# Decay exponents of a chunked delta rule: from broadcast loads and GpSimd products to sums by TensorE in PSUM

## The chip, the cores and the metric

The kernel runs on one core of a Trainium2 chip. The time is device microseconds of one launch. Three runs of the kernel before gave 1200.51, 1200.98 and 1204.93 us; the median, 1200.98 us, is the time before. One more execution was recorded by the hardware profiler: its own time is 1201.35 us, and its trace spans 1199.4 us.

## The reference, cut to what matters

One encoder layer runs over a prompt of 512 tokens and a sample of 256, each behind 16 meta tokens. The mixer has two branches: an attention branch with latent projections, and a gated delta rule that runs forward and backward over chunks of 64 tokens. A feed-forward part follows. All is float32. The change touches only the preparation of the delta rule's chunk matrices:

```python
gc = jnp.cumsum(g, axis=-1)
decay = jnp.exp(jnp.where(tri, gc[..., :, None] - gc[..., None, :], -jnp.inf))
m = jnp.where(strict, jnp.einsum('bhncd,bhnsd->bhncs', kb, k) * decay, 0.0)
attn = jnp.einsum('bhncd,bhnsd->bhncs', q, k) * decay
qg = q * jnp.exp(gc)[..., None]
```

For each chunk, head and direction a 64 x 64 matrix of differences of cumulated gates is needed, masked to a triangle and exponentiated. It multiplies k k^T (for the triangular system) and q k^T (for the local attention). q is scaled by exp(gc) as well.

## The kernel before, in words

The sequence (14 chunks of 64 columns, prompt and sample together) lies along the free axis, 128 features along the partitions. Two heads share a tile, so four pairs j = 0..3 cover the eight heads (`for j in range(NPB)`). Every float32 product of the large projections is three float32r products of a high and a low part (`proj`, L331: 48 matmuls of 384 or 400 columns per tile of 128 output features; `split`, L212 and L213, makes the parts of a weight, on ScalarE and VectorE).

The stage around the change works so, for each pair j:

- `conv` (L449 to 469) projects k and q of the pair into one two-bank PSUM tile each (pool `d2`, two tiles), ScalarE copies them to `xb`, and three VectorE steps (L465) convolve them, the result back in the same PSUM tile. `silu_pad` then applies SiLU on ScalarE (the function table is loaded again for each change between SiLU and exp/log, L184). Only then is the `d2` tile free for the next projection.
- `l2` squares (L485 on GpSimd for k, L487 on VectorE for q), sums over a head with a float32 matmul (L492, into a bank of pool `b`, three banks), and normalizes (L498, L500) to `kq`. `tokens` transposes k and stores it.
- For each half (seven chunks): two loads (L542) broadcast five lines from DRAM (`gD`: gc forward, gc backward, -beta forward, and gc of both directions with the heads swapped) over 64 partitions each, into the tile `x3` (the trace calls it x). VectorE subtracts gc of the row (L547, L548), GpSimd adds the masks (L549, L550), ScalarE takes exp of three matrices and of the two lines `en`, GpSimd multiplies by -beta (L553), VectorE by the backward one (L554). These are the four matrices `dc`.
- A matmul per chunk (L561) gives k k^T and q k^T; VectorE multiplies them by `dc` into `LT` (L566) and `ua` (L569), GpSimd multiplies `en` and q into `ua` (L568), and `ua` is stored to `UD` (L571), in two parts per half.

The lines in `gD` are made before, after the gates (L413 to 423): three times a copy, a transpose on TensorE (L417), a copy to SBUF (L419) and stores.

After the stage `LT` is transposed to `LP` (L585, L587), and 30 steps of a sequential inverse run on VectorE (`inv_steps`, L596, L598). Meanwhile the four v and four z projections (`vtok`, `zgate`) and then five latent ones go through TensorE. The v convolution writes to an SBUF tile `y` (three buffers). Then a scan over the chunks, attention, output projection and feed-forward follow.

The order on each engine isn't written by hand: a planner orders the instructions when the kernel is built, by program order as priority and by its own estimate of when each is ready, and every engine then keeps its order. All DMAs of these stages are issued by one queue, SyncE's (SP). A tile is waited for before its memory is used again, also where a later pool takes over an earlier pool's memory.

Of the kernel before, what the change touches and what calls it, by code (L numbers as in the profile page):

```python
# [5 lines left out]
F32 = mybir.dt.float32  # L6
# [27 lines left out]
def lay_consts():  # L34
    i = np.arange(128)
    c = {}
    c["ident"] = np.eye(128)
    c["J"] = np.tile(np.eye(64), (2, 1))
    c["bd1"] = np.kron(np.eye(2), np.ones((64, 64)))
    c["one"] = np.ones((128, 128))  # L40
    p = (i % 64)[:, None]
    f = np.arange(64)[None, :]
    c["tf"] = (p <= f) * 1.0
    c["tb"] = (p >= f) * 1.0
    c["nf"] = np.where(p <= f, 0.0, NEG)
    c["nb"] = np.where(p >= f, 0.0, NEG)
    s = np.zeros((128, 128))
    for m in range(128):
        r = m % 32
        s[r, m] = 1.0  # L50
        if r < 16:
            s[32 + r + 16, m] = -1.0
        else:
            s[32 + r - 16, m] = 1.0
    c["sk"] = s
    c["hm"] = np.kron(np.eye(8), np.ones((16, 64)))
    names, cols, arrs = [], {}, []
# [24 lines left out]
_C, _CC = lay_consts()


def lay(inp):

    a = {}
    a["x"] = np.concatenate([inp["meta_tokens"], inp["x_prompt"][0], inp["x_sample"][0]], 0)
    w = inp["w_in"][0]
    cq, ckv, kr, q, k, v, z, g = (np.s_[0:384], np.s_[384:640], np.s_[640:672], np.s_[672:1184],  # L90
                                  np.s_[1184:1696], np.s_[1696:2208], np.s_[2208:2720], np.s_[2720:2752])
    tiles = [np.concatenate([w[:, kr], w[:, kr], w[:, g], np.zeros((D, 32), w.dtype)], 1)]
    for j in range(4):
# [44 lines left out]
def body(ctx, tc, I, O):  # L138
# [26 lines left out]
    def bank(n="b"):  # L165
        return banks[n].tile([P, 512], F32, name=n, tag=n)
# [3 lines left out]

    def bank2():
        return banks["d2"].tile([P, 2, 512], F32, name="d2", tag="d2")
    banks_set(b=3, c=1, d2=2)

    def pool(es, name, bufs, side="right", **kw):
        return es.enter_context(tc.tile_pool(name=name, bufs=bufs, side=side, reuse_waits="tile", **kw))
# [232 lines left out]

    nbT = gqp.tile([P, 2, NCH, 4], F32, name="nbT")  # L410
    V.tensor_scalar_mul(nbT, bT, -1.0)
    gD = dp.tile([2, 5, 56, 64], F32, name="gD")
    for i, src in enumerate((gcT[:, 0], gcT[:, 1], nbT[:, 0])):  # L413
        ps = bank()
        cj = gp.tile([P, 4, NCH], F32, name="cj")
        V.tensor_copy(cj, src.rearrange("p c j -> p j c"))
        T.transpose(ps[:56, :P], cj.rearrange("p j c -> p (j c)"), ident)  # L417
        row = gp.tile([56, P], F32, name="row", bufs=2)
        S.copy(row, ps[:56, :P])  # L419
        st(gD[:, i].rearrange("h n c -> n h c"), row.rearrange("n (h c) -> n h c", h=2))  # L420
        if i < 2:
            for h in range(2):
                st(gD[h, 3 + i], row[:, (1 - h) * 64:(1 - h) * 64 + 64])
    egk = gqp.tile([P, 2, NCH, 4], F32, name="egk")
    act(egk, gcT, AF.Exp)
    ekd = gqp.tile([P, 2, NCH, 4], F32, name="ekd")
    V.tensor_sub(ekd, glT, gcT)
    act(ekd, ekd, AF.Exp)
# [18 lines left out]
    cnt = [0]  # L447

    def ytile():  # L449
        return cvp.tile([P, 803], F32, name="y", tag="y", bufs=3)  # L450

    def conv(ti, wi, eng=V, ceng=V):

# [27 lines left out]

    def l2(ks, out, scale):
        sq = sp.tile([P, GC], F32, name="sq")
        if scale is None:
            G.tensor_mul(sq, ks, ks)  # L485
        else:
            V.tensor_mul(sq, ks, ks)  # L487
        k3 = ks.rearrange("p (n c) -> p n c", c=64)
        for s in range(2):
            ps = bank()  # L490
# [34 lines left out]
    for j in range(NPB):  # L525
# [7 lines left out]
        for half in range(2):  # L533
            n0 = half * 7
            ch = slice(n0, n0 + 7)
            rows = slice(j * NCH + n0, j * NCH + n0 + 7)

            x3 = sp.tile([P, 5, 7, 64], F32, name="x3", bufs=2)
            en = x3[:, 3:5]
            for h in range(2):  # L540
                hr = slice(h * 64, h * 64 + 64)
                ld(x3[hr].rearrange("p r n c -> p r (n c)"),  # L542
                   gD[h, :, rows].rearrange("r n c -> r (n c)").partition_broadcast(64))

            dc = sp.tile([P, 4, 7, 64], F32, name="dc", bufs=2)
            gc = bc(gcT[:, :, ch, j], 3, 64)
            V.tensor_sub(dc[:, 1:4:2], x3[:, 0:2], gc)  # L547
            V.tensor_sub(dc[:, 2], gc[:, 1], x3[:, 1])  # L548
            G.tensor_add(dc[:, 1:3], dc[:, 1:3], bc(bc(C("nf"), 1, 7), 1, 2))  # L549
            G.tensor_add(dc[:, 3], dc[:, 3], bc(C("nb"), 1, 7))  # L550
            act(dc[:, 1:4], dc[:, 1:4], AF.Exp)
            act(en, en, AF.Exp)
            G.tensor_mul(dc[:, 0], x3[:, 2], dc[:, 1])  # L553
            V.tensor_mul(dc[:, 2], dc[:, 2], bc(nbT[:, 1, ch, j], 2, 64))  # L554
            b = bds[half]
            S.copy(b[0:64, :, 64:128], kq[0:64, 0, ch, :])
            S.copy(b[64:128, :, 0:64], kq[64:128, 0, ch, :])
            for a, w in ((0, 4), (4, 3)):
# [5 lines left out]
                sl = slice(a, a + w)  # L564
                nj = slice((n0 + a) * 4 + j, (n0 + a + w - 1) * 4 + j + 1, 4)
                V.tensor_mul(LT[:, :, nj, :], bc(p4[:, 0], 1, 2), dc[:, 0:4:2, sl])  # L566
                ua = sp.tile([P, 2, 4, 2, 64], F32, name="ua", bufs=3)
                G.tensor_mul(ua[:, :, :w, 0, :], en[:, :, sl], bc(kq[:, 1, n0 + a:n0 + a + w, :], 1, 2))  # L568
                V.tensor_mul(ua[:, :, :w, 1, :], bc(p4[:, 1], 1, 2), dc[:, 1:4:2, sl])  # L569
                for r in range(2):  # L570
                    st(UD[r, n0 + a:n0 + a + w, :, j].rearrange("n p i c -> p n (i c)"), ua[:, r, :w].rearrange("p n i c -> p n (i c)"))  # L571
    es.close()
    vp = pool(ec, "vp", 1)

    ei = ExitStack()
# [787 lines left out]
```

## Time and profile before

| | us |
|---|---|
| median of three runs | 1200.98 |
| the profiled execution's own time | 1201.35 |
| its span in the trace | 1199.4 |
| TensorE busy (matmuls) | 1123.9 (94%) |
| VectorE busy | 831.6 (69%) |
| ScalarE busy | 598.9 (50%) |
| GpSimd busy | 156.6 (13%) |

The shares are means over stages with different limits. A matmul's busy time holds its way through the array, so that neighbours overlap: the pace of a row of matmuls is read from the distance of their starts. The stage of the change lies between about 64 and 205 us, and the inverse follows up to 300 us. "Idle" of an engine is put down to what ended it.

### The profile page before, as it was taken

How to read it: one execution, taken by the hardware profiler on the slowest of the kernel's cores; microseconds unless marked ns; L12 is line 12 of the kernel's file. 1: busy time of each engine (PE TensorE's matmuls, PEld its weight loads, DVE VectorE, ACT ScalarE, POOL GpSimd, SP SyncE). 2: the span in 40 equal slices, each digit the busy share in tenths (PEclk: the TensorE clock that was granted, in tenths of full speed). 3: DMA queues.
4: the chain of work that ended last, by engine and by line, in shares of the span. 5: the costliest groups of instructions: out<-in, count | busy, mean ns of one | idle time of the engine just before them, and what ended most of it. 6: DMA issues, size and time to landing. Idle time of an engine off the chain costs nothing.

```text
span 1199.4 us, 18635 instructions
## 1 busy us (share of the span) xinstructions
PE 1123.9 (94%) x7116; PEld 974.5 (81%) x7116; DVE 831.6 (69%) x1358; ACT 598.9 (50%) x1054; POOL 156.6 (13%) x195
## 2 busy tenths in 40 slices
PE   5978888998999899998999899999998999999997
PEld 4877788998889876664677789999998888888885
DVE  7567668689677768778648699777764764494446
ACT  5475664333745656656534566555553533343330
POOL 2134465004513211000000000000000000000000
PEclk9998899999899989899999899999999999999999
DMA  5157764530478764334103025333324875566521
GB/s 209 50 117 182 196 171 130 126 113 31 146 253 238 214 188 124 102 98 158 45 18 106 18 71 179 129 123 123 124 88 145 306 229 177 176 206 203 179 91 52
DMA packets 107962, 168.94 MB, mean 141 GB/s; under 512 B 36242, under 2 KB 72850, under 8 KB 107874
## 3 DMA queue, kind: packets, MB, share of 16 engines
q1 hardware_dynamic: 107874, 167.76, 45.7%
q8 instruction: 56, 0.92, 0.3%
q14 instruction: 32, 0.26, 0.1%
HBM read 128.61 MB, written 39.11 MB: 140 GB/s over the span
## 4 chain that ended last, share of the span: by engine, by line
PE 77%; DVE 9%; DMA 6%; ACT 4%; issue 2%; SPq 1%; POOL 1%; DVEq 0%; ACTq 0%; POOLq 0%
PE w L1326 15%; PE w L1084 10%; PE b L1084 9%; PE d L331 7%; PE b L1326 7%; PE b L1146 5%; PE d L977 3%; PE c L1008 3%; DMA x<-gD 3%; PE b L837 2%; PE d L704 2%; PE b L853 2%; PE v L1005 2%; PE b L877 2%; PE b L870 2%
## 5 line engine op out<-in xcount | busy, mean ns | idle before, releaser
L1326 PE MATMUL w<-w2h,fh 128*128 128x512 f32 x768 | 185.1, 391 | 3.8 <-ACT fh L212 3.8
L1326 PEld LDWEIGHTS w<-w2h,fh 128*128 128x128 f32 x768 | 144.9, 189 | 34.3 <-ACT fh L212 4.1
L331 PE MATMUL d<-hTh,wl 128*128 128x384 f32 (+1 forms) x352 | 123.9, 352 | 3.3 <-DVE wl L213 3.3
L331 PE MATMUL d<-hTh,wh 128*128 128x384 f32 (+1 forms) x352 | 125.1, 355 | 1.4 <-ACT ks L188 1.4
L331 PE MATMUL d<-hTl,wh 128*128 128x384 f32 (+1 forms) x352 | 125.1, 355 | 0.0
L213 DVE TENSOR_TENSOR w2h<-LT,w2h 128x1024 fp32r<-128x1024 f32 x64 | 77.6, 1224 | 48.7 <-ACT w2h L212 48.7
L212 ACT CAST w2h<-LT 128x1024 fp32r<-128x1024 f32 x64 | 66.6, 1049 | 75.4 <-PE b L1326 28.8
L1326 PE MATMUL b<-w2h,fh 128*128 128x512 f32 x384 | 96.4, 389 | 0.0
L1326 PEld LDWEIGHTS b<-w2h,fh 128*128 128x128 f32 x384 | 72.3, 188 | 15.1
L331 PEld LDWEIGHTS d<-hTh,wh 128*128 128x128 f32 x352 | 67.6, 192 | 5.8 <-issue 3.3
L331 PEld LDWEIGHTS d<-hTh,wl 128*128 128x128 f32 x352 | 67.6, 192 | 5.8 <-DVE wl L213 3.7
L331 PEld LDWEIGHTS d<-hTl,wh 128*128 128x128 f32 x352 | 67.6, 192 | 2.6 <-issue 1.5
L213 DVE TENSOR_TENSOR fh<-fr,fh 128x768 fp32r<-128x768 f32 x32 | 30.5, 957 | 55.9 <-ACT fh L212 55.9
L212 ACT CAST fh<-fr 128x768 fp32r<-128x768 f32 x32 | 26.7, 839 | 76.0 <-PE w L1326 38.7
L212 ACT CAST w1h<-LT 128x512 fp32r<-128x512 f32 x50 | 30.8, 620 | 41.2 <-PE w L1084 20.9
L1146 PE MATMUL b<-woh,mh 128*128 128x512 f32 x96 | 42.2, 448 | 5.2 <-ACT woh L212 3.1
L977 PE MATMUL d<-kt,q 128*128 128x512 f32 (+1 forms) x96 | 46.6, 582 | 0.3 <-ACT p L188 0.2
L213 DVE TENSOR_TENSOR w1l<-LT,w1h 128x512 fp32r<-128x512 f32 x50 | 34.4, 689 | 12.6 <-ACT w1h L212 12.6
L1008 PE MATMUL c<-pt,vt 128*64 128x512 f32 (+3 forms) x96 | 42.2, 536 | 0.6 <-ACT pt L1007 0.6
L857 DVE TENSOR_TENSOR YZ<-U,b 64x512 f32<-64x512 f32 x52 | 35.5, 683 | 7.6 <-PE b L853 6.9
L834 ACT COPY YZ<-U 64x512 f32<-64x512 f32 x52 | 32.1, 617 | 17.3 <-issue 11.3
L978 DVE TENSOR_REDUCE mx<-d 128x1 f32<-128x512 f32 (+1 forms) x48 | 28.7, 599 | 16.7 <-PE d L977 16.5
(473 smaller groups left out, 2810.4 us busy)
## 6 DMA issues: line engine op xcount, KB each, us to landing
LT<-in_w_ff SPq DMA_DIRECT2D x85, 512.0 KB, 3.8
FD<-LT SPq DMA_DIRECT2D x16, 768.0 KB, 3.7
fr<-FD SPq DMA_DIRECT2D x32, 384.0 KB, 3.7
wr<-in_w_in SPq DMA_DIRECT2D x22, 512.0 KB, 3.5
x<-gD SPq DMA_DIRECT2D x16, 560.0 KB, 6.2
KV<-vD SPq DMA_DIRECT2D x26, 256.0 KB
U<-UD SPq DMA_DIRECT2D x26, 256.0 KB, 5.3
w1x<-in_w_ff SPq DMA_DIRECT2D x12, 512.0 KB, 4.5
```

The source lines that it names most:

```text
L212: S.copy(hi, src)
L213: return (eng or V).tensor_sub(lo, src, hi.bitcast(F32))
L331: T.matmul(ps[:, s, :c1 - c0], lhsT=a[:, k, :], rhs=b[:, k, c0:c1], start=(k == 0 and i == 0), stop=(k == KT - 1 and i == 2))
L704: T.matmul(ps[:, s, :HR], lhsT=a[:, k], rhs=b[:, cs], start=(k == 0 and i == 0), stop=(k == 2 and i == 2))
L834: S.copy(YZ[h][rows], U[rows, :, :, 1])
L857: V.tensor_sub(YZ[h][rows], U[rows, :, :, 0], wv[rows])
L977: T.matmul(ps[:, :w], lhsT=q[:, qs], rhs=kt[:, k0:k0 + w], start=True, stop=True)
L978: V.tensor_reduce(mx[:, 0, t:t + 1], ps[:, :w], AX.X, ALU.max)
L1008: T.matmul(po[:m, :nq], lhsT=Vs[j][:, t0 + bi, :m], rhs=pt[:, :nq], start=(bi == 0), stop=(bi == ntl - 1))
L1084: x = T.matmul(ps[:, :HR], lhsT=a[:, k, :], rhs=b[:, k, :], start=(k == 0 and i == 0), stop=(k == HQ - 1 and i == 2))
L1146: outp = T.matmul(ps, lhsT=x[:, k, :], rhs=y[:, cs], start=(k == 0 and i == 0), stop=(k == 3 and i == 2))
L1326: T.matmul(po[g][h], lhsT=a[:, i_, qs], rhs=b[:, cs], start=(n_ == 0 and j == 0), stop=(n_ == len(seq) - 1 and j == 2))
```

## The change

The lines go to DRAM as high and low float32r parts: gc of both directions, -beta forward, and now exp(gc) of both directions (`RD`, one store in place of seven). They are loaded once, not per half: `Rw` (20 lines of pair j at partitions 32j) and `Lc` (for each direction the column values of a chunk on 14 partitions, and below them an identity). Constants `dk` hold masks, signs and head selectors and are loaded once and cast. `spread` then forms each matrix of a half in a PSUM bank: for an exponent one matmul with `Lc` (its identity rows add the mask, its other rows add or subtract gc of one index) and one with selector and `Rw` (gc of the other index); for -beta and the two exp(gc) the second alone. So 6 banks and 9 matmuls of 448 columns per half. ScalarE takes exp straight from the bank, VectorE multiplies from the bank. GpSimd has no products here any more; the square of k goes to VectorE. `UD` is stored once per direction and half. Pool `b` has four banks during this stage in place of three and one of pool `c`, and the tile `y` of the v convolution moves from the pool `cvp` to `vp`, which is opened after this stage's pool is closed and takes its memory.

```diff
+def lay_decay():
+    i = np.arange(64)
+    nf = np.tile(np.where(i[:, None] <= i[None, :], 0.0, NEG), (1, 7))
+    nb = np.tile(np.where(i[:, None] >= i[None, :], 0.0, NEG), (1, 7))
+    band = np.tile(np.kron(np.eye(7), np.ones((1, 64))), (2, 1))
+    out = []
+    for sg, m in ((-1.0, nf), (1.0, nf), (-1.0, nb)):
+        a = np.zeros((128, 448))
+        a[:14] = sg * band
+        a[64:] = m
+        out.append(a)
...
-    banks_set(b=3, c=1, d2=2)
+    banks_set(d2=2, b=4)
...
-    gD = dp.tile([2, 5, 56, 64], F32, name="gD")
-    for i, src in enumerate((gcT[:, 0], gcT[:, 1], nbT[:, 0])):
...
+    RD = dp.tile([10, 2, 56, 64], F32, name="RD")
+    rows_ = gp.tile([56, 10, P], F32, name="rows_")
+    for q, src in enumerate((gcT[:, 0], gcT[:, 1], nbT[:, 0], egk[:, 0], egk[:, 1])):
+        if q % 2 == 0:
+            ps = bank()
+        src = src.rearrange("p c j -> p j c")
+        rh = gp.tile([P, 2, 4, NCH], F32R, name="rh", bufs=2)
+        V.tensor_copy(rh[:, 0], src)
+        V.tensor_sub(rh[:, 1], src, rh[:, 0].bitcast(F32))
+        for hl in range(2):
+            o = (q % 2 * 2 + hl) * P
+            T.transpose(ps[:56, o:o + P], rh[:, hl].rearrange("p j c -> p (j c)").bitcast(F32), ident)
+        if q % 2 or q == 4:
+            w = 4 if q % 2 else 2
+            S.copy(rows_[:, q // 2 * 4:q // 2 * 4 + w], ps[:56, :w * P].rearrange("n (r c) -> n r c", c=P))
+    st(RD.rearrange("r h n c -> n r h c"), rows_.rearrange("n r (h c) -> n r h c", h=2))
...
-        return cvp.tile([P, 803], F32, name="y", tag="y", bufs=3)
+        return vp.tile([P, 803], F32, name="y", tag="y", bufs=3)
...
+    dk = sp.tile([P, _D.shape[1]], F32R, name="dk")
+    for c0, c1 in ((0, 1472), (1472, 2240)):
+        raw = sp.tile([P, 1792], F32, name="dc", bufs=2)
+        ld(raw[:, :c1 - c0], I["decay"][:, c0:c1])
+        S.copy(dk[:, c0:c1], raw[:, :c1 - c0])
...
+    raw = sp.tile([P, 1792], F32, name="ua", bufs=2)[:, :896]
+    G.memset(raw, 0.0)
+    for j in range(NPB):
+        ld(raw[32 * j:32 * j + 20], RD.rearrange("r h (j n) c -> j (r h) (n c)", j=4)[j])
+    V.tensor_copy(Rw, raw)
+    for d in range(2):
+        raw = sp.tile([P, 1792], F32, name="ua", bufs=2)[:, :1024].rearrange("p (b c) -> p b c", b=8)
+        G.memset(raw, 0.0)
+        for hl in range(2):
+            for h in range(2):
+                ld(raw[hl * 7:hl * 7 + 7, :, h * 64:h * 64 + 64], RD[d * 2 + hl, h].rearrange("(b n) c -> n b c", n=7))
+        V.tensor_copy(Lc[d][0:64], raw[0:64])
+        S.copy(Lc[d][64:128], bc(dk[64:128, 1344:1472].bitcast(F32), 1, 8))
...
-        if scale is None:
-            G.tensor_mul(sq, ks, ks)
-        else:
-            V.tensor_mul(sq, ks, ks)
+        V.tensor_mul(sq, ks, ks)
...
-            V.tensor_sub(dc[:, 1:4:2], x3[:, 0:2], gc)
-            V.tensor_sub(dc[:, 2], gc[:, 1], x3[:, 1])
-            G.tensor_add(dc[:, 1:3], dc[:, 1:3], bc(bc(C("nf"), 1, 7), 1, 2))
-            G.tensor_add(dc[:, 3], dc[:, 3], bc(C("nb"), 1, 7))
-            act(dc[:, 1:4], dc[:, 1:4], AF.Exp)
-            act(en, en, AF.Exp)
-            G.tensor_mul(dc[:, 0], x3[:, 2], dc[:, 1])
+            def spread(i, d=None, r=None):
+                ps = bank()
+                if d is not None:
+                    T.matmul(ps[:, :448], lhsT=Lc[d][:, 2 * j + half, :], rhs=dkr[r], start=True, stop=False)
+                T.matmul(ps[:, :448], lhsT=dks[i][rs_], rhs=Rw[rs_, half * 448:half * 448 + 448],
+                         start=d is None, stop=True)
+                return ps[:, :448].rearrange("p (n c) -> p n c", c=64)
...
+            act(dc[:, 1], spread(0, 0, 0), AF.Exp)
+            V.tensor_mul(dc[:, 0], dc[:, 1], spread(3))
+            act(dc[:, 2], spread(2, 1, 1), AF.Exp)
             V.tensor_mul(dc[:, 2], dc[:, 2], bc(nbT[:, 1, ch, j], 2, 64))
+            act(dc[:, 3], spread(1, 1, 2), AF.Exp)
+            ua = sp.tile([P, 1792], F32, name="ua", bufs=2).rearrange("p (r n i c) -> p r n i c", r=2, n=7, c=64)
+            for r in range(2):
+                V.tensor_mul(ua[:, r, :, 0, :], kq[:, 1, ch, :], spread(4 + r))
...
-                G.tensor_mul(ua[:, :, :w, 0, :], en[:, :, sl], bc(kq[:, 1, n0 + a:n0 + a + w, :], 1, 2))
-                V.tensor_mul(ua[:, :, :w, 1, :], bc(p4[:, 1], 1, 2), dc[:, 1:4:2, sl])
-                for r in range(2):
-                    st(UD[r, n0 + a:n0 + a + w, :, j].rearrange("n p i c -> p n (i c)"), ua[:, r, :w].rearrange("p n i c -> p n (i c)"))
+                V.tensor_mul(ua[:, :, sl, 1, :], bc(p4[:, 1], 1, 2), dc[:, 1:4:2, sl])
+            for r in range(2):
+                st(UD[r, n0:n0 + 7, :, j].rearrange("n p i c -> p n (i c)"), ua[:, r].rearrange("p n i c -> p n (i c)"))
     es.close()
+    banks_set(d2=2, b=3, c=1)
     vp = pool(ec, "vp", 1)
```

## Rows read from the trace of the kernel before

**Rows 1.** Busy time of each engine by stretch, granted clock, DMA share; columns named first.
```profile
core 0: us, PE busy (x) PEld busy (x) DVE busy (x) ACT busy (x) POOL busy (x), PEclk, DMA share, GB/s
64.00:205.00 141.00, 119.63 (x622) 109.28 (x622) 100.30 (x118) 87.39 (x149) 72.60 (x56) 0.90 0.67 163
205.00:262.00 57.00, 57.00 (x353) 56.70 (x352) 40.37 (x54) 21.28 (x36) 5.56 (x15) 1.00 0.48 125
262.00:300.00 38.00, 34.80 (x194) 33.90 (x192) 37.10 (x40) 13.58 (x22) 13.18 (x14) 1.00 0.14 46
300.00:420.00 120.00, 111.39 (x1706) 103.28 (x1706) 86.09 (x135) 70.48 (x134) 40.09 (x62) 0.96 0.70 213
```
**Rows 2.** Chain that ended last, 40 to 350 us, in order of time.
```profile
64.31 2.20 DMA gD<-row
68.55 12.69 DMA x<-gD
```
**Rows 3.** Waits between 64 and 205 us: us in total, times, longest.
```profile
DVE dc L547 <- DMA x<-gD: 23.3, 7, 6.6
ACT x L188 <- DMA x<-gD: 9.5, 5, 2.9
```
**Rows 4.** TensorE in order of time: starts that give the pace of 384 and 400 columns.
```profile
102.51 0.33 PE L331 MATMUL d<-hTl,wh 128*128 128x384 f32 x1
...
105.82 0.34 PE L331 MATMUL d<-hTh,wl 128*128 128x384 f32 x1
...
106.36 0.34 PE L331 MATMUL d<-hTl,wh 128*128 128x400 f32 x1
...
109.63 0.34 PE L331 MATMUL d<-hTl,wh 128*128 128x400 f32 x1
```
**Rows 5.** Groups of TensorE, 64 to 205 us: busy us, mean ns, idle before.
```profile
L561 PE MATMUL b<-kq,bd 128*128 128x128 f32 x112 | 19.9, 341 | 3.8 <-DVE ua L569 1.5 <-DVE kq L498 1.4 <-ACT kt L508 0.9
L492 PE MATMUL b<-sq,cst 128*128 128x448 f32 x32 | 15.2, 567 | 2.5 <-DVE kq L500 2.5
```
**Rows 6.** Groups of VectorE, 64 to 205 us.
```profile
L213 DVE TENSOR_TENSOR wl<-wr,wh 128x1024 fp32r<-128x1024 f32 x8 | 16.2, 2022 | 1.3 <-ACT wh L212 1.3
L465 DVE SCALAR_TENSOR_TENSOR y<-xb,cols,y 128x803 f32<-128x803 f32 x9 | 10.9, 1212 | 0.3 <-ACT y L462 0.2
L554 DVE TENSOR_TENSOR dc<-dc,nbT 128x448 f32<-128x448 f32 x8 | 10.0, 1251 | 3.5 <-ACT dc L188 3.4
L547 DVE TENSOR_TENSOR dc<-x,gcT 128x896 f32<-128x896 f32 x8 | 8.7, 1092 | 25.2 <-DMA x<-gD 23.3 <-issue 1.9
L548 DVE TENSOR_TENSOR dc<-gcT,x 128x448 f32<-128x448 f32 x8 | 5.2, 644 | 0.0
```
**Rows 7.** VectorE in order of time: single instructions at either duration, and LT's last.
```profile
88.02 0.61 DVE L554 TENSOR_TENSOR dc<-dc,nbT 128x448 f32<-128x448 f32 x1
...
123.24 1.21 DVE L213 TENSOR_TENSOR wl<-wr,wh 128x1024 fp32r<-128x1024 f32 x1
...
154.03 0.61 DVE L498 SCALAR_TENSOR_TENSOR kq<-ks,b 128x448 f32<-128x448 f32 x1
...
202.22 0.55 DVE L566 TENSOR_TENSOR LT<-b,dc 128x384 f32<-128x384 f32 x1
```
**Rows 8.** Groups of ScalarE, 64 to 205 us.
```profile
L188 ACT ACTIVATE dc<-dc 128x1344 f32<-128x1344 f32 x8 | 10.6, 1323 | 1.8 <-POOL dc L549 1.7
L188 ACT ACTIVATE b<-b 128x448 f32<-128x448 f32 x16 | 8.4, 542 | 0.0
L188 ACT ACTIVATE x<-x 128x896 f32<-128x896 f32 x8 | 7.7, 956 | 9.5 <-DMA x<-gD 9.5
```
**Rows 9.** DMA issues, 64 to 205 us: count, KB each, median us to landing.
```profile
x<-gD SPq DMA_DIRECT2D x16, 560.0 KB, 6.2
vD<-kt SPq DMA_DIRECT2D x16, 112.0 KB, 4.8
```
**Rows 10.** TensorE in order of time: the sums for one q tile.
```profile
141.99 1.67 PE L492 MATMUL b<-sq,cst 128*128 128x448 f32 x4
```

More of the change, by code (lines that the diff above doesn't have):

```diff
@@ L44, in lay_consts @@
     c["tb"] = (p >= f) * 1.0
-    c["nf"] = np.where(p <= f, 0.0, NEG)
-    c["nb"] = np.where(p >= f, 0.0, NEG)
     s = np.zeros((128, 128))
@@ L63, in lay_consts @@
     return np.concatenate(arrs, 1).astype(np.float32), cols
+def lay_decay():
[9 more added lines that the diff above has]
+        out.append(a)
+    a = np.zeros((128, 128))
+    a[64:] = np.tile(np.eye(64), (1, 2))
+    out.append(a)
+    head = np.arange(128) // 64
+    for q, sg, swap in ((0, 1.0, 0), (1, 1.0, 0), (1, -1.0, 0), (2, 1.0, 0), (3, 1.0, 1), (4, 1.0, 1)):
+        a = np.zeros((128, 128))
+        for j in range(4):
+            for hl in range(2):
+                for h in range(2):
+                    a[32 * j + (q * 2 + hl) * 2 + h] = sg * (head == (1 - h if swap else h))
+        out.append(a)
+    return np.concatenate(out, 1).astype(np.float32)
 def rope_tables():
@@ L82 @@
 _C, _CC = lay_consts()
+_D = lay_decay()
 def lay(inp):
@@ L124, in lay @@
     a["consts"] = _C
+    a["decay"] = _D
     a["rope"] = rope_tables()
@@ L411, in body @@
     V.tensor_scalar_mul(nbT, bT, -1.0)
-    gD = dp.tile([2, 5, 56, 64], F32, name="gD")
-    for i, src in enumerate((gcT[:, 0], gcT[:, 1], nbT[:, 0])):
[L414 to L423, printed above, removed]
     egk = gqp.tile([P, 2, NCH, 4], F32, name="egk")
     act(egk, gcT, AF.Exp)
+    RD = dp.tile([10, 2, 56, 64], F32, name="RD")
[14 more added lines that the diff above has]
+    st(RD.rearrange("r h n c -> n r h c"), rows_.rearrange("n r (h c) -> n r h c", h=2))
     ekd = gqp.tile([P, 2, NCH, 4], F32, name="ekd")
@@ L473, in body @@
     sp = pool(es, "sp", 1)
+    dk = sp.tile([P, _D.shape[1]], F32R, name="dk")
[3 more added lines that the diff above has]
+        S.copy(dk[:, c0:c1], raw[:, :c1 - c0])
+    dkr = [dk[:, i * 448:(i + 1) * 448] for i in range(3)]
+    dks = [dk[:, 1472 + i * P:1472 + (i + 1) * P] for i in range(6)]
+    Rw = sp.tile([P, 896], F32R, name="Rw")
+    Lc = [sp.tile([P, 8, P], F32R, name=f"Lc{d}") for d in range(2)]
+    raw = sp.tile([P, 1792], F32, name="ua", bufs=2)[:, :896]
[6 more added lines that the diff above has]
+        G.memset(raw, 0.0)
+        for hl in range(2):
+            for h in range(2):
+                ld(raw[hl * 7:hl * 7 + 7, :, h * 64:h * 64 + 64], RD[d * 2 + hl, h].rearrange("(b n) c -> n b c", n=7))
+        V.tensor_copy(Lc[d][0:64], raw[0:64])
+        S.copy(Lc[d][64:128], bc(dk[64:128, 1344:1472].bitcast(F32), 1, 8))
     def silu_pad(y, ks):
@@ L535, in body @@
             ch = slice(n0, n0 + 7)
[L536 to L546, printed above, removed]
-            V.tensor_sub(dc[:, 1:4:2], x3[:, 0:2], gc)
-            V.tensor_sub(dc[:, 2], gc[:, 1], x3[:, 1])
-            G.tensor_add(dc[:, 1:3], dc[:, 1:3], bc(bc(C("nf"), 1, 7), 1, 2))
-            G.tensor_add(dc[:, 3], dc[:, 3], bc(C("nb"), 1, 7))
-            act(dc[:, 1:4], dc[:, 1:4], AF.Exp)
-            act(en, en, AF.Exp)
-            G.tensor_mul(dc[:, 0], x3[:, 2], dc[:, 1])
+            rs_ = slice(32 * j, 32 * j + 20)
+            def spread(i, d=None, r=None):
[5 more added lines that the diff above has]
+                return ps[:, :448].rearrange("p (n c) -> p n c", c=64)
+            dc = sp.tile([P, 1792], F32, name="dc", bufs=2).rearrange("p (q n c) -> p q n c", q=4, c=64)
+            act(dc[:, 1], spread(0, 0, 0), AF.Exp)
+            V.tensor_mul(dc[:, 0], dc[:, 1], spread(3))
+            act(dc[:, 2], spread(2, 1, 1), AF.Exp)
             V.tensor_mul(dc[:, 2], dc[:, 2], bc(nbT[:, 1, ch, j], 2, 64))
+            act(dc[:, 3], spread(1, 1, 2), AF.Exp)
+            ua = sp.tile([P, 1792], F32, name="ua", bufs=2).rearrange("p (r n i c) -> p r n i c", r=2, n=7, c=64)
+            for r in range(2):
+                V.tensor_mul(ua[:, r, :, 0, :], kq[:, 1, ch, :], spread(4 + r))
             b = bds[half]
@@ L566, in body @@
                 V.tensor_mul(LT[:, :, nj, :], bc(p4[:, 0], 1, 2), dc[:, 0:4:2, sl])
-                ua = sp.tile([P, 2, 4, 2, 64], F32, name="ua", bufs=3)
-                G.tensor_mul(ua[:, :, :w, 0, :], en[:, :, sl], bc(kq[:, 1, n0 + a:n0 + a + w, :], 1, 2))
-                V.tensor_mul(ua[:, :, :w, 1, :], bc(p4[:, 1], 1, 2), dc[:, 1:4:2, sl])
-                for r in range(2):
-                    st(UD[r, n0 + a:n0 + a + w, :, j].rearrange("n p i c -> p n (i c)"), ua[:, r, :w].rearrange("p n i c -> p n (i c)"))
+                V.tensor_mul(ua[:, :, sl, 1, :], bc(p4[:, 1], 1, 2), dc[:, 1:4:2, sl])
+            for r in range(2):
+                st(UD[r, n0:n0 + 7, :, j].rearrange("n p i c -> p n (i c)"), ua[:, r].rearrange("p n i c -> p n (i c)"))
     es.close()
+    banks_set(d2=2, b=3, c=1)
     vp = pool(ec, "vp", 1)
```

## The prediction

> **What bounds the kernel now.** I read the busy time by stretch first [rows 1]. In the stage of the change (64 to 205 us) TensorE is busy 119.6 of 141 us, VectorE 100.3, ScalarE 87.4, GpSimd 72.6, and the DMA engines 67% of the time. TensorE has the most work, but here it isn't saturated: 21.4 us of idle, and a granted clock of 0.90. Behind it, from 205 to 262 us, it has no idle at all, and from 262 to 300 us VectorE (37.1 of 38) and TensorE (34.8) are both nearly full. From 300 to 420 us TensorE idles 8.6 of 120 us. So over 64 to 420 us TensorE has 33 us of idle, two thirds of it in this stage. The reader should take from it that only idle of TensorE is to be had, and that work added to TensorE is paid for nearly in full, unless it falls into that idle.
>
> Then the chain and the waits. In the stage the chain passes through the broadcast loads, the first time for 12.7 us, right behind the landing of the lines in DRAM [rows 2]. Within the stage VectorE waits 23.3 us and ScalarE 9.5 us for these loads [rows 3]. Both engines keep their order, so these waits hold up what stands behind: the normalization of k and q, the convolutions, SiLU, and with it the two `d2` banks that the next projection needs. That is where TensorE's 21.4 us come from: its idle before L561 and L492 ends with VectorE or ScalarE [rows 5], not with a DMA.
>
> **What goes.** Of VectorE: L547 8.7 and L548 5.2 us [rows 6]. Also a stretching: L213 takes 2.02 us in the mean against 1.21 alone, L554 1.25 against 0.61 [rows 6, 7]; over 8 each that is 6.5 + 5.1 = 11.6 us, and the long ones lie beside GpSimd's products, which go. The Trainium skill, "SBUF — State Buffer", section "SBUF: two separate sides", says why: a VectorE operation with two SBUF inputs and a GpSimd operation exclude each other for a whole instruction. By that rule, which these durations bear out, all 11.6 us come back, and the new products that read PSUM as one input can't be caught so.
> Of ScalarE: the exp of three matrices (10.6) and of the lines (7.7) [rows 8]. Of GpSimd nearly all of its 72.6 us. Of the DMA 16 x 560 KB [rows 9], and SP's queue is free of loads that wait for a tile.
>
> **What comes.** TensorE: 6 matrices of 9 matmuls per half, 8 halves, 72 matmuls of 448 columns. None of this shape with float32r is in the trace. 384 columns go at (105.82 - 102.51)/19 = 0.174 us, 400 at (109.63 - 106.36)/18 = 0.182 [rows 4]; by the slope 448 take 0.205. From below the cost is 0 (all of it in today's idle of 21.4 us), from above that of a float32 sum of 448 columns, which is recorded as two matmuls of 0.567 us mean [rows 5]: 72 x 0.567 = 40.8. I take 72 x 0.205 = 14.8, since the projections have the same type and nearly the length. Seven more transposes of lines stand in front of the stage, where TensorE is full: between 0 and 7 x 0.341 (the mean of a 128-column record [rows 5]) = 2.4; I take 1.0.
> VectorE: per half three products from a bank, 0.61 each as L498 [rows 7]: 14.6 us; the square of k, 4 x 1.1 as L547 of the same size: 4.4; casts and subtractions of the lines and tiles about 4. Sum: 100.3 - 13.9 - 11.6 + 23.0 = 97.8. ScalarE: 24 exps of 448 from a bank, 0.542 each [rows 8]: 13.0, and some 4 of casts, against 18.3: 86. Both stay below TensorE's work, so they cost nothing by their sums; where they are late, TensorE waits, and that is what I price as idle.
> The tile `y` moves behind this stage: the three convolutions of v that are done in the stage today (nine steps, 10.9 us [rows 6]) fall past the end of `LT`. VectorE has 57 - 40.4 = 16.6 us of idle between 205 and 262 us [rows 1], which hides them; without that cover they lengthen the inverse by as much. TensorE can still project four v tiles ahead (two `d2` tiles, two `xb`), so it doesn't starve on it.
> The new loads: one store, four loads of `Rw`, eight of `Lc`, the second `Lc` only after `Rw` is cast (both use the two `ua` buffers). The store has 280 KB in pieces of 256 B. Nearest rows: the old store landed in 2.2 us (28 KB) [rows 2], a store of k in the same pieces in 4.8 (112 KB) [rows 9]. Bounds: 2.2, or 2.5 x 4.8 = 12; I take 5.5. With 12 issues of half a microsecond, a landing and the casts the lines are there some 15 us after their last copy (about 63 us), at 78 us; between 72 and 87 by the bounds. Today's first loads end their part of the chain at 81.2 [rows 2]. So the first pair gains little, the other three no longer wait.
> "DMA: Bandwidth & Descriptors", section "Specifications", of the Trainium skill speaks against this part: pieces below 512 B don't reach line rate. The store of k agrees: a fifth of a broadcast load's bytes takes three quarters of its time [rows 9]. By that rule I would take 12 us for the store, and it makes the second rival below.
>
> **The sum.** Profiled execution 1201.35 (span 1199.4 and 1.95 around it; 0.4 above the median of the runs, which I neglect).
> +14.8 for the sums, +1.0 for the transposes.
> -13.4: idle in the stage from 21.4 to 8. Of the first pair's idle, before the lines arrive, I leave half of about 8 us; for each of the 8 halves I add 0.5 us in which TensorE waits for a bank that a product of 0.61 us has to empty.
> -4: lower clock. 0.90 granted over 141 us between the levels 1.2 and 2.4 GHz means 28 us at the lower one [rows 1]; 21.4 us of idle take part of that, so between 3.4 and 14 us of work time are lost. I take 6, and 2 after: between 205 and 300 us, where TensorE has little idle, the clock is 1.00 [rows 1].
> -3.9: a third of the 11.8 us of idle between 262 and 420 us [rows 1]: `LT` is ready earlier, the inverse ends earlier against TensorE's backlog of projections.
> Sum -5.5: 1195.9, say **1196**. What is late next is TensorE itself.
>
> **The rivals.**
> (a) Shorter chain: `LT` is complete at 202.8 us [rows 7]. TensorE's work for the four pairs alone, without the three v projections it does ahead (3 x 48 x 0.178 = 25.6 us), is 119.6 - 25.6 + 14.8 = 109; `LT` could be done by 175. If what follows is bound by the chain rather than by TensorE, 28 us less arrive early and VectorE's 10.9 us of v convolutions come back: 1201.35 - 17.1 = 1184. For it: the inverse is one chain on VectorE. Against: no idle of TensorE from 205 to 262 us.
> (b) The lines come late: 6.5 us later, by the bound of the store. TensorE, out of `d2` banks, idles that long in the first pair: 1196 + 6 = 1202, no change.
> (c) Banks: pool `b` was taken 10 times per pair, now 22 times (4 sums, 2 transposes, 4 products, 12 matrices). 88 uses of 4 banks in 141 us allow 6.4 us each; from a longer mean on the stage is longer than today. A bank of one q sum was held from 141.99 to 154.6 us [rows 7, 10], 12.6 us. At 7 us in the mean the stage takes 88 x 7 / 4 = 154 us: 1201 + 13 = 1214, slower. Against it: this hold contains a wait for a load that goes, and a matrix needs its bank only for a matmul and one exp or product of 0.6 us.
>
> **How the numbers follow.** Mine 0.48 (1189 to 1201 by its own bounds), (a) 0.18, (b) 0.17, (c) 0.17. No change means within 0.5%, 6 us, about what a measurement of this kernel can tell. Mine splits into 0.24 faster and 0.24 same; (a) is faster; (b) 0.11 same and 0.06 slower; (c) 0.02 same and 0.15 slower. Faster 0.42, same 0.37, slower 0.21. The range 1181 to 1213 leaves out the outer half of (c) and the far side of (a).
>
> **What would show it.** Right: no waits for a load on VectorE after the first pair, L213 at 1.2 us throughout, GpSimd nearly empty, matmuls of 448 columns at 0.2 us, TensorE's idle in the stage below 10 us, its clock above 0.95. Wrong: idle of TensorE before the new matmuls, ended by ScalarE or VectorE (banks, c); VectorE waiting long for the cast of `Rw` or `Lc` (b); TensorE with idle behind `LT` although projections are left, which would mean that v convolutions held by `y` cost what I hide.

## The result and the profile after

The changed kernel takes 1241.17 us (median of 4 runs, 1237.51 to 1243.09); the kernel before took 1202.17 beside it (4 runs). The ratio is 1.0318, 95% interval 1.0285 to 1.0352: slower, where I had forecast 1196 and a range up to 1213. The profiled execution took 1243.09, its span 1241.3.

By stretch, with the columns of [rows 1]:

```profile
64.00:205.00 141.00, 138.47 (x663) 116.62 (x662) 82.62 (x116) 79.15 (x153) 2.20 (x13) 0.93 0.35 93
205.00:262.00 57.00, 54.23 (x316) 51.24 (x315) 42.78 (x63) 20.72 (x36) 6.32 (x14) 0.97 0.39 104
262.00:300.00 38.00, 38.00 (x215) 37.65 (x214) 36.69 (x30) 13.59 (x20) 10.64 (x5) 1.00 0.30 89
300.00:420.00 120.00, 110.88 (x1579) 103.16 (x1577) 83.76 (x126) 64.83 (x118) 42.26 (x63) 0.94 0.57 178
```

GpSimd is empty and the DMA share is halved, as meant. TensorE's idle in the stage is 2.5 us, and it isn't fast: it is busy 18.8 us more than before.

VectorE from 64 to 205 us, groups: busy, mean ns, idle before. The first two answer to L213 and L554 of [rows 6]:

```profile
L239 DVE TENSOR_TENSOR wl<-wr,wh 128x1024 fp32r<-128x1024 f32 x9 | 11.0, 1225 | 9.7 <-ACT wh L238 9.1 <-PE d L357 0.5
...
L601 DVE TENSOR_TENSOR dc<-dc,nbT 128x448 f32<-128x448 f32 x7 | 4.3, 620 | 0.0
```

The stretching beside GpSimd is gone: 1225 ns for 2022, 620 for 1251. What is left of waits for loads there, in place of the 23.3 us of [rows 3] (us in total, times, longest):

```profile
DVE Rw L518 <- DMA ua<-RD: 3.0, 1, 3.0
...
DVE Lc L525 <- DMA ua<-RD: 1.2, 1, 1.2
```

TensorE from 64 to 216 us: the new sums (L593 with 20 rows of weights, L592 with 128), and L612, which answers to L561 of [rows 5]:

```profile
L593 PE MATMUL b<-Rw,dk 20*128 20x448 f32 x48 | 20.5, 477 | 0.0
L612 PE MATMUL b<-kq,bd 128*128 128x128 f32 x112 | 19.5, 343 | 0.1
...
L592 PE MATMUL b<-dk,Lc 128*128 128x448 f32 x24 | 11.0, 459 | 2.4 <-DVE ua L618 2.1 <-ACT dc L214 0.3
```

The sums take 20.5 + 11.0 = 31.5 us as recorded. Recorded durations overlap with their neighbours, so this isn't yet what they cost; my 14.8 was a price by starts. In order of time, matmuls first (start us, us), then the loads of their weights, with the idle before each:

```profile
123.91 0.47 PE L592 MATMUL b<-dk,Lc 128*128 128x448 f32 x1
124.31 0.46 PE L593 MATMUL b<-Rw,dk 20*128 20x448 f32 x1
124.70 0.47 PE L592 MATMUL b<-dk,Lc 128*128 128x448 f32 x1
```
```profile
123.91 0.19 PEld L592 LDWEIGHTS b<-dk,Lc 128*128 128x128 f32 x1 [0.30 <-issue]
124.31 0.18 PEld L593 LDWEIGHTS b<-Rw,dk 20*128 20x128 f32 x1 [0.21 <-issue]
124.70 0.19 PEld L592 LDWEIGHTS b<-dk,Lc 128*128 128x128 f32 x1 [0.21 <-issue]
```

They start 0.39 to 0.40 us apart here, at a granted clock of 1.00; of all 56 pairs of neighbouring sums none is under 0.28. The load sits idle 0.21 us, which is one matmul of this length, and then takes 0.19: load and matmul stand one behind the other. In the projections just ahead, loads of 0.19 us start every 0.17 to 0.19 us, each beside the matmul before it.

The stage isn't all, though. `LT`'s last product starts 12.6 us later than before (214.8 for 202.2 [rows 7]), and the span ends 41.9 us later. The rest comes up behind it, and attention shows where: the first product of the values (L1008 before, L1058 after) starts at 451.5 us before and at 546.1 after, while the first scores are late by 25 us only (450.3 for 424.9). Its row before and after (duration min, median, max in ns, then first and last start):

```profile
L1008 PE MATMUL c<-pt,vt x96: 377/592/697, 451.5 to 621.0; 128*64 128x512 f32 x32, 128*128 128x512 f32 x32, 128*64 128x256 f32 x16, 128*128 128x256 f32 x16
```
```profile
L1058 PE MATMUL c<-pt,vt x96: 377/592/1116, 546.1 to 659.7; 128*64 128x512 f32 x32, 128*128 128x512 f32 x32, 128*64 128x256 f32 x16, 128*128 128x256 f32 x16
```

What runs just ahead of it on TensorE is the last sum of the scan's output norm (L946, into pool `b`):

```profile
545.12 1.06 PE L946 MATMUL b<-sq,cst 128*128 128x512 f32 x1
546.11 4.22 PE L1058 MATMUL c<-pt,vt 128*64 128x512 f32 x8
```

### The profile page after: what moved, and what is told of

It is laid out like the page before. It is cut to its first block, busy times and chain, and to the rows that moved or that the text cites. A ratio compares the mean times of both kernels' runs of the same rounds, so it can differ in the third digit from the quotient of the medians.

```text
span 1241.3 us, 18759 instructions
## 1 busy us (share of the span) xinstructions
PE 1160.7 (94%) x7195; PEld 993.9 (80%) x7195; DVE 827.3 (67%) x1380; ACT 597.5 (48%) x1066; POOL 92.6 (7%) x154
## 4 chain that ended last, share of the span: by engine, by line
PE 80%; DVE 11%; ACT 4%; DMA 3%; issue 2%; SPq 0%; POOL 0%; DVEq 0%; ACTq 0%
PE d L357 15%; PE w L1376 14%; PE w L1134 10%; PE b L1134 9%; PE b L1376 7%; PE b L1196 4%; PE d L1027 3%; PE c L1058 3%; PE d L754 2%; PE b L887 2%; PE v L1055 1%; PE b L903 1%; PE b L612 1%; PE b L927 1%; PE b L542 1%
## 5 line engine op out<-in xcount | busy, mean ns | idle before, releaser
L238 ACT CAST wh<-wr 128x1024 fp32r<-128x1024 f32 x22 | 23.2, 1052 | 48.3 <-PE d L357 43.4
L239 DVE TENSOR_TENSOR w1l<-LT,w1h 128x512 fp32r<-128x512 f32 x50 | 34.4, 690 | 12.6 <-ACT w1h L238 12.6
L1058 PE MATMUL c<-pt,vt 128*64 128x512 f32 (+3 forms) x96 | 41.5, 549 | 0.9 <-ACT pt L1057 0.6
```

Source lines behind the costliest of these rows:

```text
L238: S.copy(hi, src)
L239: return (eng or V).tensor_sub(lo, src, hi.bitcast(F32))
L1058: T.matmul(po[:m, :nq], lhsT=Vs[j][:, t0 + bi, :m], rhs=pt[:, :nq], start=(bi == 0), stop=(bi == ntl - 1))
```

## The experiments

Three causes were taken one after the other: where PSUM pools stand, the price of a sum, and the place of `y`. The first is read from the addresses of the tiles in the built kernels. A pool takes its banks only when a tile of it is made; attention makes no tile of `b` until late, so after the change it has this layout (e1, e2 and e5 are the first, second and fourth run below):

```
            scan                        attention
before      b 0-2, c 3, d2 4-7          b 0-2 (kept), d 3-4, v 5-6, c 7
changed     d2 0-3, b 4-6, c 7          d 0-1, v 2-3, c 4
e1          as the changed kernel       as the changed kernel
e2          as before                   as before
e5          d2 0-3, c 4, b 5-7          d 0-1, v 2-3, c 4
```

**Attention's own order.**
```diff
-    banks_set(b=3, d=2, v=2, c=1)
+    banks_set(d=2, v=2, b=3, c=1)
```


> The changed kernel with one line different, far behind the stage: attention takes its PSUM pools in the order d, v, b, c instead of b, d, v, c, so that scores and values use the banks of the latents (0 to 3) and not those of the scan (4 to 6). Theory P (pool order): the values, which start at 546.1 us now and at 451.5 in the kernel before, start again during the scan, near 465; of the 42 us lost some 28 come back: 1213 us (1207 to 1219). Rival S (the stage and its late start carry the whole loss, and the values are late for another reason, as the transfers or the order of the planner): within 6 us of 1241. Both agree on the stage itself: LT complete at 215 us as now.

1238.95 us, ratio 1.0314 (1.0276 to 1.0351): no change, and the values still start at 541.9 us. My theory had the wrong pools. The table shows why: `b` is empty in attention, so the order of the names does nothing. What collides is `c` on bank 4.

**The old order from the end of the stage on.**
```diff
     es.close()
-    banks_set(d2=2, b=3, c=1)
+    banks_set(b=3, c=1, d2=2)
```


> The changed kernel with its second order of PSUM pools b, c, d2 (that of the kernel before) in place of d2, b, c, from the end of the stage on. Theory P: attention keeps b on banks 0 to 2 and finds d, v and c on banks that the latents have left; the same gain as with attention's own order, 1213 us (1207 to 1219), values from about 465 us. Rival S: within 6 us of 1241. A second rival, that moving b onto the old d2 banks at the end of the stage holds up LP's copies: 2 to 5 us less of the gain than attention's own order shows.

1225.11 us, ratio 1.0193 (1.0161 to 1.0225): 15 us of the 28, by the ratios. The values start at 494.4 us. The layout matters, but the scores come later than in the changed kernel (from 459 us for 450), which is more than the second rival had for LP's copies.

**The kernel before with the new order.**
```diff
-    banks_set(b=3, c=1, d2=2)
+    banks_set(d2=2, b=3, c=1)
```


> The kernel before, with nothing changed but the order in which it takes its first PSUM pools: d2, b, c in place of b, c, d2 (the sizes are the same). Theory P: the first values wait for the end of the scan, from 451 to about 539 us, and the kernel loses 25 to 30 us: 1228 us (1222 to 1233). Rival S: 1202, within 4 us. The stage from 64 to 205 us is as before under both.

1225.94 us, ratio 1.0190 (1.0151 to 1.0229). One line with nothing of the change costs 1.9%:

```profile
L1008 PE MATMUL c<-pt,vt x96: 378/592/1057, 532.3 to 645.4; 128*64 128x512 f32 x32, 128*128 128x512 f32 x32, 128*64 128x256 f32 x16, 128*128 128x256 f32 x16
```

The last sum of the scan's output norm starts at 531.8 us there, and the values stand behind it again.

**c alone.**
```diff
     es.close()
-    banks_set(d2=2, b=3, c=1)
+    banks_set(d2=2, c=1, b=3)
```


> The run with attention's own order left every tile of PSUM on the bank that it had: a pool gets banks at its first tile, b has none in attention, so that c stands on bank 4 in both, and bank 4 is one of the scan's (b on 4 to 6). Theory C (it is c, the accumulator of the values, that collides): with the order d2, c, b after the stage c has bank 4, the scan has 5 to 7, and attention's d, v and c (0 to 4) meet none of the scan's. The values start near 477 us (31 us behind the first scores, as before) and not at 546; 1213 us (1207 to 1219). Rival S (it isn't the banks; the second order b, c, d2 helped by moving the inverse): within 6 us of 1241.

1224.72 us, ratio 1.0167 (1.0128 to 1.0206), and the values start where expected:

```profile
L1058 PE MATMUL c<-pt,vt x96: 378/592/697, 479.3 to 640.0; 128*64 128x512 f32 x32, 128*128 128x512 f32 x32, 128*64 128x256 f32 x16, 128*128 128x256 f32 x16
```

So it is `c`: attention's accumulator of the values shared a bank with the scan. It is worth 1.5%, some 18 us, not my 28; the values are still 28 us later than before, about as much as the scores, so that this rest comes from ahead of attention. The next kernels build on this one.

**Casts on GpSimd** (built on the second run).
```diff
-        S.copy(dk[:, c0:c1], raw[:, :c1 - c0])
+        G.tensor_copy(dk[:, c0:c1], raw[:, :c1 - c0])
...
-        S.copy(Lc[d][64:128], ...)
+        G.tensor_copy(Lc[d][64:128], ...)
```


> As the run with the second pool order b, c, d2, and besides the casts of the masks and selectors (dk) and of the identity rows of Lc on GpSimd instead of ScalarE. Theory: the gates are late by 5.5 us because ScalarE spends 4.3 us of the layer norm's time on these casts; off ScalarE the gates are ready near 46 us and the end is 4 to 6 us earlier than with the pool order alone: 1208 us if that is 1213. Rival: ScalarE has room there and the lateness has another cause (the load of 1.1 MB ahead of the weights, seven more transposes): within 2 us of the pool order alone.

1229.91 us, ratio 1.0217 (1.0171 to 1.0264): not better than without it. ScalarE in order of time, the second run and this one:

```profile
39.93 0.48 ACT L372 COPY graw<-d 32x400 f32<-32x400 f32 x1
...
41.31 0.34 ACT L382 COPY gt<-b 128x224 f32<-128x224 f32 x1 [0.40 <-PE b L380]
```
```profile
36.28 0.48 ACT L372 COPY graw<-d 32x400 f32<-32x400 f32 x1
...
42.92 0.35 ACT L382 COPY gt<-b 128x224 f32<-128x224 f32 x1 [3.53 <-PE b L380]
```

The casts did hold the layer norm up, by 3.7 us at the first copy of the gates. But the planner then put the gates' transposes behind a projection, and the copy that needs them is 1.6 us later, not earlier.

**Weights of 128 rows.** A copy of the selectors per pair, zero outside the pair's 20 rows:
```diff
+        dj = sp.tile([P, 6, P], F32R, name="dj", bufs=2)
+        G.memset(dj.bitcast(F32), 0.0)
+        G.tensor_copy(dj[32 * j:32 * j + 20]..., dk[32 * j:32 * j + 20, 1472:2240]...)
...
-                T.matmul(ps[:, :448], lhsT=dks[i][rs_], rhs=Rw[rs_, half * 448:half * 448 + 448],
+                T.matmul(ps[:, :448], lhsT=dj[:, i], rhs=Rw[:, half * 448:half * 448 + 448],
```


> As the run with c on bank 4, and the selectors of the new sums taken over all 128 rows instead of 20 (a copy for each pair with zeros elsewhere, made on GpSimd). Theory W: the sums start 0.40 us apart, twice the 0.205 forecast, because a load of weights for 20 rows behind a matmul of 128 rows, and the other way round, waits for the matmul before it; with one size the loads are hidden and the pace is 0.20 to 0.22 us: 72 x 0.2 = 14 us less TensorE work, LT ready some 12 us earlier, the end 8 to 14 us earlier than with c on bank 4 alone. Rival B: it is the change of PSUM bank with each sum, or the type, and the pace stays 0.40: within 3 us of c on bank 4.

1210.65 us, ratio 1.0061 (1.0041 to 1.0082). The last product of `LT` starts at 200.9 us, 12.4 earlier than with c on bank 4 alone. Matmuls and loads of one half, and the stage:

```profile
120.44 0.36 PE L595 MATMUL b<-dk,Lc 128*128 128x448 f32 x1
120.64 0.37 PE L596 MATMUL b<-Rw,dj 128*128 128x448 f32 x1
120.85 0.36 PE L595 MATMUL b<-dk,Lc 128*128 128x448 f32 x1
121.05 0.37 PE L596 MATMUL b<-Rw,dj 128*128 128x448 f32 x1
```
```profile
120.64 0.19 PEld L595 LDWEIGHTS b<-dk,Lc 128*128 128x128 f32 x1
120.85 0.19 PEld L596 LDWEIGHTS b<-Rw,dj 128*128 128x128 f32 x1
```
```profile
64.00:205.00 141.00, 132.76 (x714) 118.76 (x714) 85.03 (x122) 83.58 (x158) 9.65 (x26) 0.99 0.38 105
```

The loads start with the matmul before them, and the pace is 0.20 to 0.21 us, as I had taken from the projections: 26 of the 56 pairs of neighbouring sums lie there, where the changed kernel has none. The others stand behind the first sum of a row (0.28 to 0.32), at the lower clock (0.37, below), or wait for a bank or an operand. The clock is 0.99.

**All sums with 20 rows.**
```diff
-                    T.matmul(ps[:, :448], lhsT=Lc[d][:, 2 * j + half, :], rhs=dkr[r], start=True, stop=False)
...
+                    T.matmul(ps[:, :448], lhsT=dks[i][rs_], rhs=Rw[rs_, half * 448:half * 448 + 448],
+                             start=False, stop=True)
...
-            act(dc[:, 1], spread(0, 0, 0), AF.Exp)
+            act(dc[:, 1], spread(0, 0, 0), AF.Exp, scale=1e-9)
```


> As the run with c on bank 4, and the 24 sums with 128-row weights replaced by a second sum with 20-row weights (this leaves the columns' lines and the masks out, and the exps get a scale of 1e-9 so that nothing overflows): all 72 matmuls stay, all with 20 rows. Theory M (the array drains when the number of rows of the tile changes from one matmul to the next): where no bank is waited for, the sums start 0.20 to 0.21 us apart, as with full rows, and only the first of a row of them, behind a projection or a product of 128 rows, waits; 1211 us (1206 to 1216). Rival K (a load for 20 rows is never hidden behind a matmul): 0.40 us for every sum, and 1225 (1221 to 1230).

1208.92 us, ratio 1.0040 (1.0015 to 1.0064). Loads of weights at the start of one half (the matmuls start at 117.87, 118.18 and 118.39 us): the first waits, behind a matmul of 128 rows, the next don't.

```profile
117.87 0.18 PEld L591 LDWEIGHTS b<-Rw,dk 20*128 20x128 f32 x1 [0.25 <-issue]
117.98 0.18 PEld L594 LDWEIGHTS b<-Rw,dk 20*128 20x128 f32 x1
118.19 0.39 PEld L591 LDWEIGHTS b<-Rw,dk 20*128 20x128 f32 x2
```

Of the 53 pairs of neighbouring sums 17 start 0.20 to 0.21 us apart; behind the first sum of a row it is 0.31, and at the lower clock (below) 0.37. The run leaves the masks and the columns' lines out, so only its time and order count. So 20 rows are no obstacle; the step between 20 and 128 rows is. The Trainium skill, "TensorEngine Tiling (Array Packing)", section "Key Properties", has the rule: changing the tiling mode, not merely the tile, drains TensorE. The runs agree, if 20 and 128 rows count as two modes, which is my reading: 0.40 us a sum where the sizes take turns, 0.20 where they don't and nothing else is waited for, for weights of either size.

**y in the stage's time.**
```diff
     def ytile():
-        return vp.tile([P, 803], F32, name="y", tag="y", bufs=3)
+        return cvp.tile([P, 803], F32, name="y", tag="y", bufs=2)
```


> As the run with c on bank 4, and the tile y of the convolutions of v back in the pool that lives through the stage, in two buffers (before: three). Theory: TensorE is full in the stage, so that it makes no difference where the projections of v run: within 3 us of c on bank 4. Rival: VectorE's 10.9 us of convolutions of v, which the forecast hid behind LT, lengthen the inverse: 5 to 10 us earlier than c on bank 4 alone.

1207.87 us, ratio 1.0035 (1.0018 to 1.0051), better than either theory had it: 1.3% off the run with c on bank 4. It isn't VectorE's convolutions: the last step of the inverse starts at 308.8 us, with c on bank 4 alone at 308.5. The difference shows in TensorE's idle and clock behind the stage, c on bank 4 first, then this run (columns of [rows 1]):

```profile
205.00:262.00 57.00, 54.33 (x319) 51.43 (x319) 44.45 (x65) 21.95 (x38) 6.33 (x14) 0.97 0.36 96
300.00:420.00 120.00, 111.92 (x1573) 104.69 (x1571) 82.51 (x126) 65.60 (x119) 40.96 (x62) 0.91 0.58 178
```
```profile
205.00:262.00 57.00, 57.00 (x359) 56.81 (x358) 40.59 (x60) 18.86 (x34) 6.23 (x14) 1.00 0.41 116
300.00:420.00 120.00, 115.49 (x1706) 108.05 (x1704) 91.23 (x143) 73.16 (x137) 42.85 (x68) 0.96 0.66 202
```

2.7 and 3.6 us more work there, and a clock of 1.00 and 0.96 for 0.97 and 0.91. The 2.7 us stood before the transposes of `LT` to `LP` (L635), which waited five times for their copies by VectorE (L637). But a late `y` doesn't have to bring this about. The run with 20 rows throughout has `y` behind the stage too, and its TensorE is as full:

```profile
205.00:262.00 57.00, 57.00 (x356) 56.74 (x355) 46.10 (x65) 21.11 (x37) 6.27 (x14) 1.00 0.43 116
300.00:420.00 120.00, 114.83 (x1717) 107.11 (x1718) 91.85 (x144) 74.08 (x140) 44.41 (x70) 0.97 0.68 210
```

So the time of that run holds more than the pace of its sums, and that it met theory M's range is in part luck.

**Only y in the kernel before.**
```diff
-        return cvp.tile([P, 803], F32, name="y", tag="y", bufs=3)
+        return vp.tile([P, 803], F32, name="y", tag="y", bufs=3)
```


> The kernel before, with only the tile y of the convolutions of v moved behind the stage, as the change does (three buffers, no other edit). Theory Y: the projections of v are held until LT is done, and TensorE has idle and a lower clock behind the stage: 10 to 20 us slower, 1212 to 1222. Rival: in the kernel before the stage has 21 us of idle anyway, so y costs what the forecast hid, at most VectorE's 10.9 us of convolutions, and likely nothing: 1202 to 1207.

1206.13 us, ratio 1.0029 (1.0015 to 1.0044). The move costs 0.3% by itself, the rival's size. TensorE has the same idle behind the stage as with c on bank 4 (54.67 of 57 us busy from 205 to 262 us, clock 0.97), and yet loses 4 us here for 16 there; why isn't shown.

**The three together.** The full rows and `y` on top of c on bank 4; the tile of k's tokens shares its buffer with the squares, for room.
```diff
-        tokens(..., sp.tile([P, GC], F32, name="kt"), j, 0, bank)
+        tokens(..., sp.tile([P, GC], F32, name="kt", tag="sq"), j, 0, bank)
```


> The three edits together: c on bank 4, selectors over 128 rows, y in the pool of the stage in two buffers (to make room, the tile of k's tokens shares its buffer with the squares). If the three costs are separate they add up: 1241 - 16.5 - 14 - 17 = 1194 us (1189 to 1199), faster than the kernel before. Rival: the 14 us of the selectors and the 17 us of y are the same idle and clock of TensorE, won back twice: 1205 (1202 to 1210).

1203.18 us (12 runs), ratio 1.0006 (0.9992 to 1.0019). They don't add up: this is the rival's range. From 300 to 420 us TensorE has idle again (108.7 us busy, clock 0.91; this execution took 1209.0 and is the longest of the 12).

**Late casts,** on top of the three.
```diff
-    S.copy(gt, ps[:, :224]...)
+    gtc = S.copy(gt, ps[:, :224]...)
...
-        S.copy(dk[:, c0:c1], raw[:, :c1 - c0])
+        i = S.copy(dk[:, c0:c1], raw[:, :c1 - c0])
+        tc.add_manual_dep(i.ins, gtc.ins.name, NOSYNC, reason="behind the gates")
```


> As the three edits together, and the two casts of the masks and selectors ordered behind the copy of the gates' transposes on ScalarE, so that they don't stand in the layer norm. Theory: the gates, 5.5 us late in the changed kernel, come back to 45 us, and the end comes 3 to 6 us earlier than with the three edits. Rival: the planner places other work in the gap, as it did when GpSimd made the casts (gates at 53.1 us): within 2 us of the three edits, or later.

1204.16 us (12 runs), ratio 1.0012 (0.9997 to 1.0027). The edit changed nothing: with the three edits alone both casts already stand behind that copy (at 40.2 and 41.5 us, the copy at 39.6), and every engine has its instructions in the same order in both built kernels. So this is the kernel of the run before once more, and the theory wasn't tested. That the gates come at 48.5 us here, 1.6 earlier, goes with the clock of this one execution (1.00 for 0.54 from 24 to 30 us). What late gates cost (44.8 us in the kernel before) isn't shown.

## Why the prediction was wrong

In steps, by the ratios to the kernel before: 3.18% as changed, 1.67 with `c` off the scan's bank, 0.61 with full rows, 0.06 with `y` back. Of 1202 us that makes 18, 13 and 7 us. The order matters, since full rows and `y` share part of theirs: taken first, `y` is worth 16. Under 1 us of the loss is left over, and nothing of a gain. With full rows, and with `y` back, the planner also put ScalarE's casts behind the gates (`dk` at 40.3 and 39.5 us for 17.8 with c on bank 4 alone), and the SiLU of the first q came 2.0 and 1.3 us earlier; up to that much of the 13 and 16 us can be this.

**What bounds the kernel, and what goes: right.** TensorE was the bound, waits for loads went, and VectorE's stretching with them. By the Trainium skill, "SBUF — State Buffer", section "SBUF: two separate sides", that was to be expected with GpSimd's products gone, and 2022 to 1225 ns bears it out. The rows that I cited for TensorE's idle [rows 5] hold only 6.3 of the 21.4 us; the largest part, 10.4, stood before L507 (transposes), but ended with ScalarE or VectorE too, so the reading holds. VectorE's 97.8 us still held the 10.9 of v convolutions that I moved out of the stage one paragraph on; 82.6 were measured, and nothing hung on it.

**What comes: this step failed, in three places.**
- PSUM banks: it has no term for the two lines of `banks_set`, though they stand in the diff. I read them as a fourth bank for the stage. They also turn the order of the pools round, and with it the bank that attention's `c` gets 350 us later. Rival (c) asked how long a bank is held within the stage; those waits of TensorE were 2.4 us. Nearly half of the loss is this.
- 72 sums at 0.205 us: the price was that of a matmul among others of its size. 24 of the sums have 128 rows of weights and 48 have 20, mixed, and a change costs the load that is hidden otherwise. At 0.40 they make 72 x 0.40 = 28.8 (31.5 as recorded), within my upper bound of 40.8. I took the row that was nearest in length and type; it has neighbours of its own size, and the sums don't.
- `y` at no cost: I had looked for VectorE's 10.9 us, which were indeed hidden. What I passed over is TensorE, of which I wrote that it doesn't starve. With `y` alone put back 16 us return, and with them TensorE's idle and clock between 205 and 420 us; the idle behind `LT` that I had named as a sign of this did come (54.23 of 57 us busy). That it costs about this much in this kernel is shown; how it does isn't, since the run with 20 rows throughout has `y` as late and no such idle.

One smaller term held, and one came out near by luck. The store of the lines was issued at 71.3 us and the loads behind it from 74.8, 3.5 us later, within my 2.2 to 12 and far from the 12 that I gave for the rule in "DMA: Bandwidth & Descriptors", section "Specifications", of the Trainium skill. But their last copy ended at 71.2 us where I had 63, and the last cast (the second `Lc`) at 83.7 where I had 78, within my 72 to 87: a start 8 us late was in part made up behind it. ScalarE's casts, at nothing in the sum, hold the layer norm up by 3.7 us; what that costs in the end no run shows.

**The sum.** Idle in the stage 8 us: it was 2.5 in the changed kernel, because the sums had filled it, and 8.2 with full rows (141 - 132.76). The clock above 0.95: 0.93, and 0.99 with full rows. So the stage came out as forecast once its sums had the price that I gave them. But `LT`'s last product then starts at 200.9 us, for 202.2 before. The stage starts later (SiLU of the first q at 69.0 us with full rows, for 66.2), and what it won in idle and clock went to the sums. Of the 3.9 us further back 3.6 came: between 262 and 420 us TensorE idles 8.2 us with full rows (120 - 111.85, and nothing up to 300) for 11.8 before [rows 1]. But 2.4 us of new idle between 205 and 262 us (57 - 54.58), and a clock of 0.93 for 0.96 from 300 to 420, stand against it.

**The rivals.** (c) had the right sign and the wrong mechanism. (a) did not occur. In (b) the lines came late, by 5.7 us for its 6.5, though not by the store; but TensorE didn't idle for it, with 2.5 us of idle in the whole stage.

Open is why the old order from the end of the stage on delays the scores, and why `y` costs 4 us in the kernel before, 7 behind full rows and 16 ahead of them; the planner's order differs in each of these kernels, and no run held it fixed. Open too is what the lower clock (below) is worth by itself: the run with 20 rows throughout has it and is as fast as that with full rows, but it leaves `Lc`'s part out, so the two can't be set against each other.

## What to carry to other kernels

Read every line of a diff that names a pool as a move of addresses, and follow each tile to the next stage that lands on its bank; the price can come due hundreds of microseconds later. Price a matmul by its neighbours, not by its length: small weights between large ones cost a load each time. And when an engine is the bound, ask of every buffer that is moved which of its work can no longer run ahead.

## What the runs showed of the hardware

TensorE's clock fell behind the sums with 20 rows, though TensorE was hardly idle. The changed kernel behind the second half of the first pair, in steps of 2 us (columns of [rows 1]):

```profile
94.00:96.00 2.00, 0.96 (x4) 0.39 (x3) 2.00 (x4) 0.55 (x1) 0.00 (x0) 1.00 0.00 0
96.00:98.00 2.00, 2.00 (x6) 1.19 (x6) 2.00 (x5) 1.64 (x3) 0.00 (x0) 0.68 0.03 10
98.00:100.00 2.00, 2.00 (x10) 2.00 (x10) 2.00 (x5) 1.99 (x4) 0.00 (x0) 0.50 1.02 286
100.00:102.00 2.00, 2.00 (x9) 1.99 (x9) 2.00 (x5) 1.72 (x3) 0.00 (x0) 0.50 0.57 163
102.00:104.00 2.00, 2.00 (x9) 1.98 (x8) 1.17 (x2) 0.00 (x0) 0.00 (x0) 0.61 0.44 127
```

Half of full speed is the lower level, 1.2 GHz. Ahead of the fall TensorE did the sums of two halves with 1.04 us of idle among them. Over the stage the clock was 0.93 with 48 of 72 sums at 20 rows, 0.90 with all 72, and 0.99 with none, although TensorE had more idle in that last run (8.2 us for 2.5). The other runs bear this out only in part: 0.99 in all three with full rows, but 0.84 to 0.94 among those with 48 of 72, so that more such sums don't simply mean a lower clock. So idle isn't all that the clock follows here; the waits for loads aren't either, since they were gone with 20 rows throughout but for the first sum of a row. What it does follow was not settled.
